# Plain block products for the first five feed-forward chunks, with the operand sums beside them

## The chip, the cores and the metric

One core of a Trainium2 chip runs the whole program in one launch. A time is the device time of that core in microseconds; the kernel before was timed three times, and once more under the profiler. Of the engines, TensorE (PE) multiplies matrices into PSUM, VectorE (DVE) and ScalarE (ACT) do the elementwise work, GpSimd (POOL) helps them, and SyncE (SP) issues nearly all transfers.

## What is computed

A two-layer encoder over two token streams (1024 and 256 tokens, each with 16 meta tokens ahead): layer 0 mixes tokens with a long convolution, layer 1 with attention. After each mixer comes a layer norm of the residual sum, and then the part that this change touches, a convolutional gated feed-forward block:

```python
def conv_ffn(x, w_in, conv_w, conv_b, w_out):
    h = x @ w_in                                  # 1024 -> 2 x 2816
    g, a = jnp.split(h, 2, axis=-1)
    g = dwconv3(g, conv_w, conv_b)                # width 3 over positions
    return (jax.nn.gelu(g, approximate=False) * a) @ w_out

def run_trunk(...):
    ...
        h = layer_norm(DEEPNORM_ALPHA * h + m, ln1_g[i], ln1_b[i])
        f = conv_ffn(h, ffn_w_in[i], ffn_conv_w[i], ffn_conv_b[i], ffn_w_out[i])
        h = layer_norm(DEEPNORM_ALPHA * h + f, ln2_g[i], ln2_b[i])
```

All is float32. The kernel keeps that accuracy by splitting each operand into a high and a low part (`split`: ScalarE rounds a copy, VectorE subtracts it) and adding three matmuls, high times high, high times low and low times high (`mm3`).

## The kernel before

Activations lie transposed, channels on partitions in 8 blocks of 128 (`KC`), tokens along the free axis. The tokens of both streams together are cut into four windows, which form two **pairs**: pair 0 has two windows of 384 tokens, pair 1 two of 272 (layer 0) or 258 (layer 1). A window carries one neighbour at each side for the convolution, so its matmuls have 386, 274 or 260 columns (`n2`). Within a pair the windows are c = 0 and c = 1.

**`out_proj`** is the mixer's output projection with the residual. For pair 0 and then pair 1 it takes 8 chunks `m` of 128 output channels, with 48 matmuls each, and adds the residual on VectorE. When a pair is through, its **`window_norms`** is put on a list of background generators. `tick(us)` runs a background generator on by one step whenever the foreground has emitted about that much matmul time; `need(key)` runs a generator to its end. So the list decides in which order work is *written*; each engine then executes its own queue in order. In the written order a recording layer makes small moves; where the result matters it is shown below.

`window_norms` normalises both windows of a pair (VectorE subtracts the mean and scales, ScalarE squares and adds the bias, GpSimd sums the squares, TensorE sums over partitions), stores them to `xd`, and makes the **operands** of the feed-forward product.

**`ffn_in`** computes `h` in 22 chunks of 128 hidden channels (`MF`); chunk m needs 128 columns of the gate half and 128 of the value half of `w_in`. For one pair that is a two by two block product: left the weight quarters a11, a12 (gate, input channels 0 to 511 and 512 to 1023) and a21, a22 (value), right the blocks B11, B21 (window 0, lower and upper channels) and B12, B22 (window 1). It is done with seven products in place of eight (`PRODUCTS`). The right operands are B11, B21, B22 and the sums T2, T1, T3, T4; the left ones are the quarters and sums of them, which `left_operands` forms on VectorE (four additions of 128x512 per chunk, L935 to L940) and splits (seven per chunk). A product has 4 blocks x 3 = 12 matmuls, so a chunk has 84 matmuls per pair. The products are added up partly in PSUM, partly by VectorE (L997, L1002, L1004) after a ScalarE copy (L995); then come the convolution (`conv3`, L315 to L317), Gelu, the multiplication by the value half and the store to `hd` (L989, L991).

The **order of chunks** is the list `jobs`. Chunks 0 to 3 (`FIRST = 4`) are done for pair 0 alone, then for pair 1 alone, and each of the two rounds loads and splits its weights for itself; chunks 4 to 21 are done for both pairs with one set of weights. While the first four run for pair 0, the ticks drive the norms and operands of pair 1.

Buffers that matter: weight quarters land in four tiles `raw`, their split parts take eight tiles `w`, so four split left operands exist at a time; `tp` has nine tiles, PSUM six banks for products. The stores, the loads of weights and the stores of normalised activations are all issued from SP's one queue. `ffn_out` follows and reads `hd` back.

## Time and profile before

| what | us |
|---|---|
| median of three runs (lowest to highest) | 3580.74 (3579.64 to 3582.94) |
| the profiled execution: its own time | 3577.93 |
| the profiled execution: span of the trace | 3575.6 |
| feed-forward input phase of layer 0, first to last matmul | 989.3 to 1584.8 |
| feed-forward input phase of layer 1, first to last matmul | 2631.1 to 3212.7 |

The page of the profile gives busy time by engine, then the span in 40 slices, then the transfer queues, the chain of work that ended last, and the costliest groups of instructions. A group's row has the source line, the engine, the operation, output and inputs by the program's names, shape and count, and then busy time and the mean of one in ns. In a timeline row the first two numbers are start and duration in us, and a bracket at the end gives how long the engine had been idle and what released it. A row of the stage view gives the stretch, its length, busy time of each engine with the number of instructions, the clock granted to TensorE (1.00 is full), and the transfer engines' share and rate. Matmuls overlap in the records: their cost in a row of them is the distance from start to start.

### The profile page before, as it was taken

What the parts mean: (1) busy time and instruction counts of PE and PEld (TensorE: products, weight loads), DVE (VectorE), ACT (ScalarE), POOL (GpSimd) and SP (SyncE); (2) the same over time, 40 slices, a digit from 0 to 9 for tenths busy, and PEclk for the clock granted to TensorE, in tenths of its full rate; (3) what the DMA queues carried; (4) which work ended last, traced back from release to release, by engine and by line L of the source; (5) the groups of instructions that cost most, each with busy time, mean ns of one, the idle gap of its engine ahead of it and who ended that gap; (6) DMA issues with size and microseconds to landing.
All of it is one profiled execution on the core that took longest, in us unless ns stands there. A gap on an engine that the chain in (4) does not pass through costs nothing.

```text
span 3575.6 us, 61608 instructions
## 1 busy us (share of the span) xinstructions
PE 3415.6 (96%) x23000; PEld 3307.6 (93%) x23000; DVE 2296.8 (64%) x4631; ACT 1708.4 (48%) x3614; POOL 523.8 (15%) x651
## 2 busy tenths in 40 slices
PE   8999999998989999999999999999988999999996
PEld 7999999998979999999999988888978999999996
DVE  6555554665797666654677557776499666664566
ACT  4333333663465444433455447777275444443454
POOL 2434341111110000000102341110110000000110
PEclk8999999999999999999999999999999999999998
DMA  5222223544223221236565440000233222227585
GB/s 167 94 94 95 91 83 120 145 134 149 93 85 99 63 75 62 75 125 212 169 212 166 140 141 16 14 14 25 92 114 100 67 74 64 75 82 227 165 224 141
DMA packets 236927, 391.72 MB, mean 110 GB/s; under 512 B 30580, under 2 KB 130139, under 8 KB 236243
## 3 DMA queue, kind: packets, MB, share of 16 engines
q1 hardware_dynamic: 228051, 359.38, 32.6%
q0 software_dynamic: 8576, 28.39, 2.2%
q8 instruction: 181, 2.97, 0.3%
q14 instruction: 119, 0.97, 0.1%
HBM read 302.22 MB, written 78.84 MB: 107 GB/s over the span
## 4 chain that ended last, share of the span: by engine, by line
PE 63%; DVE 6%; ACT 3%; DMA 3%; issue 1%; POOL 0%; SPq 0%; POOLq 0%; ACTq 0%; DVEq 0%
PE mm L288 17%; PE mm L290 17%; PE mm L289 17%; PE pt L1270 2%; DMA hraw<-hd 1%; PE sc L288 1%; DVE w L260 1%; PE pv L1286 1%; PE pv L1287 1%; PE pv L1288 1%; PE sc L289 1%; PE sc L290 1%; DVE T L260 1%; PE rs L1277 1%; DMA raw<-in_w_fin 1%
## 5 line engine op out<-in xcount | busy, mean ns | idle before, releaser
L288 PE MATMUL mm<-T,w 128*128 128x386 f32 (+2 forms) x2464 | 778.1, 316 | 34.0 <-ACT w L259 26.6
L290 PE MATMUL mm<-T,w 128*128 128x386 f32 (+2 forms) x2464 | 775.1, 315 | 3.9 <-DVE w L260 3.6
L260 DVE TENSOR_TENSOR w<-raw,w 128x512 fp32r<-128x512 f32 (+2 forms) x744 | 514.6, 694 | 410.7 <-ACT w L259 397.8
L289 PE MATMUL mm<-T,w 128*128 128x386 f32 (+2 forms) x2464 | 774.5, 314 | 0.0
L259 ACT CAST w<-raw 128x512 fp32r<-128x512 f32 (+2 forms) x744 | 438.9, 593 | 693.4 <-PE mm L289 531.8
L288 PE MATMUL mm<-y,w 128*128 128x386 f32 (+6 forms) x1664 | 545.4, 328 | 13.4 <-ACT y L259 9.4
L290 PE MATMUL mm<-y,w 128*128 128x386 f32 (+6 forms) x1664 | 532.0, 320 | 12.9 <-DVE w L260 12.8
L289 PE MATMUL mm<-y,w 128*128 128x386 f32 (+6 forms) x1664 | 533.4, 321 | 1.8 <-POOL y L260 1.1
L288 PEld LDWEIGHTS mm<-T,w 128*128 128x128 f32 x2464 | 468.3, 190 | 41.6 <-ACT w L259 31.1
L290 PEld LDWEIGHTS mm<-T,w 128*128 128x128 f32 x2464 | 468.0, 190 | 7.9 <-DVE w L260 7.7
L289 PEld LDWEIGHTS mm<-T,w 128*128 128x128 f32 x2464 | 468.9, 190 | 0.3
L288 PE MATMUL mm<-hq,w 128*128 128x328 f32 (+2 forms) x1408 | 441.2, 315 | 9.7 <-ACT hq L259 9.7
L289 PE MATMUL mm<-hq,w 128*128 128x328 f32 (+2 forms) x1408 | 441.3, 313 | 0.2
L290 PE MATMUL mm<-hq,w 128*128 128x328 f32 (+2 forms) x1408 | 441.0, 313 | 0.0
L790 POOL TENSOR_TENSOR tp<-tp,tp 128x384 f32<-128x384 f32 (+4 forms) x105 | 115.3, 1110 | 1753.7 <-ACT tp L788 1749.2
L288 PEld LDWEIGHTS mm<-y,w 128*128 128x128 f32 x1664 | 322.3, 194 | 18.4 <-ACT y L259 12.2
L290 PEld LDWEIGHTS mm<-y,w 128*128 128x128 f32 x1664 | 322.4, 194 | 14.5 <-DVE w L260 14.1
L289 PEld LDWEIGHTS mm<-y,w 128*128 128x128 f32 x1664 | 322.2, 194 | 7.9 <-DVE y L260 3.5
L288 PEld LDWEIGHTS mm<-hq,w 128*128 128x128 f32 x1408 | 266.7, 190 | 10.9 <-ACT hq L259 10.9
L289 PEld LDWEIGHTS mm<-hq,w 128*128 128x128 f32 x1408 | 267.9, 190 | 1.6 <-DVE hq L260 1.3
L290 PEld LDWEIGHTS mm<-hq,w 128*128 128x128 f32 x1408 | 267.5, 190 | 0.0
L260 DVE TENSOR_TENSOR hq<-hraw,hq 128x656 fp32r<-128x656 f32 (+1 forms) x220 | 188.8, 858 | 53.3 <-ACT hq L259 50.5
(213 smaller groups left out, 5770.8 us busy)
## 6 DMA issues: line engine op xcount, KB each, us to landing
raw<-in_w_fin SPq DMA_DIRECT2D x208, 256.0 KB
hraw<-hd SPq DMA_DIRECT2D x110, 328.0 KB
hraw<-hd SPq DMA_DIRECT2D x110, 321.0 KB
raw<-in_w_fout SPq DMA_DIRECT2D x88, 256.0 KB
hd<-g SPq DMA_DIRECT2D x88, 192.0 KB
raw<-in_w_fout SPq DMA_DIRECT2D x88, 192.0 KB
raw<-in_w_hin SPq DMA_DIRECT2D x48, 256.0 KB
kk<-kd SPq DMA_DIRECT2D x64, 192.0 KB
```

Source lines behind the costliest of these rows:

```text
L259: self.nc.scalar.copy(out=h, in_=src)
L260: (self.nc.gpsimd if pool else self.nc.vector).tensor_tensor(out=l, in0=src, in1=h, op=ALU.subtract)
L288: mm(out=ps, lhsT=wh, rhs=xh, start=start and i == 0, stop=False, **skip)
L289: mm(out=ps, lhsT=wh, rhs=xl, start=False, stop=False, **skip)
L290: mm(out=ps, lhsT=wl, rhs=xh, start=False, stop=stop and i == last, **skip)
L790: (adder or nc.gpsimd).tensor_tensor(out=sm, in0=sm, in1=sq, op=ALU.add)
L1270: nc.tensor.transpose(pt[:kn, q0:q0 + m], pr[:m, 128 * j:128 * j + kn], self.ident[:m, :m])
L1277: nc.tensor.matmul(out=rs[:, q0:q0 + m], lhsT=sm[:m, 3:4].to_broadcast([m, 128]), rhs=self.ident[:m, :m], start=True, stop=True)
L1286: mm(out=pv, lhsT=vh, rhs=ph[:kn, :nn], start=(jj == 0), stop=False)
L1287: mm(out=pv, lhsT=vh, rhs=pl[:kn, :nn], start=False, stop=False)
L1288: mm(out=pv, lhsT=vl, rhs=ph[:kn, :nn], start=False, stop=last)
```

## The change

Pair 0's first chunks are now five (`FIRST = 5`), and they are computed with **plain products**: gate and value rows, each for both windows, eight blocks of three matmuls into one bank, thus 4 x 24 = 96 matmuls per chunk. They need only B11, B21, B12 and B22 and no sums, on either side. Weight quarters are split as they come (`parts(quarter_of(...))`, four splits a chunk); the convolution reads PSUM directly, and nothing is added up outside PSUM.

`window_norms` of pair 0 therefore ends with 16 plain splits. The sums and splits for T2, T1 and T3 become a background generator of their own, `rest`, which runs by ticks during the five plain chunks; T4, which lies in the buffers of the activations (tag `y0`, where B12 was), is written after the fifth chunk (`end0`). Pair 1's norms and operands run in the background as before, with the same operations in another order.

Pair 1's chunks 0 to 4 no longer come in one row after pair 0's. `AFTER` puts each of them, alone, behind one of the chunks that are done for both pairs: chunk 0 behind 7, 1 behind 10, 2 behind 13, 3 behind 16, 4 behind 19. Chunks 5 to 21 are done for both pairs.

```diff
-FIRST = 4
+FIRST = 5
+AFTER = {FIRST + 2 + 3 * i: i for i in range(FIRST)}
...
+        if p == 0:
+            for x, src in (("B11", A[0][:4]), ("B21", A[0][4:]), ("B12", A[1][:4]), ("B22", A[1][4:])):
+                for k in range(4):
+                    if k % 2 == 0:
+                        operand(x, k // 2)
+                    put(x, k, src[k])
+                    yield 1
+
+            def rest():
+                for k in range(4):
+                    if k % 2 == 0:
+                        for x in ("T2", "T1", "T3"):
+                            operand(x, k // 2)
+                    sums(k)
+                    yield 3
+
+            def end():
+                for k in range(4):
+                    if k % 2 == 0:
+                        operand("T4", k // 2)
+                    put("T4", k, A[0][k + 4])
+                    yield 1
+
+            self.later("rest", rest())
+            self.end0 = end()
...
-        jobs = [(m, (p,)) for p in range(2) for m in range(FIRST)] + [(m, (0, 1)) for m in range(FIRST, MF)]
+        jobs = []
+        for m in range(FIRST, MF):
+            jobs.append((m, (0, 1)))
+            if m in AFTER:
+                jobs.append((AFTER[m], (1,)))

         def operands():
+            for m in range(FIRST):
+                for x in (w[m], w[MF + m]):
+                    yield 2, self.parts(self.quarter_of(x[:, 0:4])) + self.parts(self.quarter_of(x[:, 4:8]))
             for m, _ in jobs:
-                yield from self.left_operands(...)
+                for x in self.left_operands(...):
+                    yield 1, x
...
+        self.need(0)
+        for m in range(FIRST):
+            g = [self.tp(n) for _ in range(2)]
+            for row in range(2):
+                wt = weights()
+                for c, (x, y) in enumerate((("B11", "B21"), ("B12", "B22"))):
+                    ps = bank()[:, :n2]
+                    self.mm3(ps, [(*wt[k], *(z[:, k % 2] for z in T[x if k < 4 else y][k % 4 // 2])) for k in range(KC)])
+                    if row == 0:
+                        self.conv3(g[c], ps, n, self.cwf[:, l, m])
+                        nc.scalar.activation(out=g[c], in_=g[c], func=AF.Gelu)
+                    else:
+                        store(0, c, m, g[c], ps[:, 1:n + 1])
+                    self.tick(0.011 * n2)
+        self.need("rest")
+        for _ in self.end0:
+            pass
```

The order on the engines shows the move. **VectorE, layer 0, the last two chunks of pair 1's output projection.** T are right operands (T1905 and T1906 are high and low part of B11), A the normalised activations, tp sums, w the low parts of split weights (w1924 and w1927 before, w1910 and w1913 now, belong to output chunk 6), mm the product banks. Before:

```order
L260 TENSOR_TENSOR T1908_9580<-A1744_8477,T1907_9579 128x386
L906 TENSOR_TENSOR tp1920_9594<-A1752_8485,tp1919_9593 128x386
L260 TENSOR_TENSOR T1910_9582<-tp1919_9593,T1909_9581 128x386
L769 TENSOR_TENSOR tp1831_9042<-tp1831_9042,A1827_9038 128x274
L260 TENSOR_TENSOR T1912_9584<-tp1920_9594,T1911_9583 128x386
L911 TENSOR_TENSOR tp1919_9593<-A1744_8477,tp1919_9593 128x386
L260 TENSOR_TENSOR T1914_9586<-A1748_8481,T1913_9585 128x386
L260 TENSOR_TENSOR w1924_9642<-raw1922_9639,w1923_9641 128x512
L260 TENSOR_TENSOR T1916_9588<-A1752_8485,T1915_9587 128x386
L260 TENSOR_TENSOR w1927_9648<-raw1925_9645,w1926_9647 128x512
```

Now:

```order
L262 TENSOR_TENSOR T1906_9578<-A1740_8473,T1905_9577 128x386
L857 SCALAR_TENSOR_TENSOR A1827_9038<-A1827_9038,mm1907_9582 128x274
L262 TENSOR_TENSOR T1906_9578<-A1741_8474,T1905_9577 128x386
L771 TENSOR_TENSOR tp1831_9042<-tp1831_9042,A1827_9038 128x274
L262 TENSOR_TENSOR w1910_9614<-raw1908_9611,w1909_9613 128x512
L262 TENSOR_TENSOR T1916_9652<-A1742_8475,T1915_9651 128x386
L262 TENSOR_TENSOR w1913_9620<-raw1911_9617,w1912_9619 128x512
L262 TENSOR_TENSOR T1916_9652<-A1743_8476,T1915_9651 128x386
L262 TENSOR_TENSOR w1920_9688<-raw1918_9685,w1919_9687 128x512
```

Before, a whole block of sums and splits for the seven operands stood ahead of the two weight splits; now w1910 has two splits of B11 ahead of it, and w1913 one more.

**VectorE, layer 0, the first weights of the feed-forward block.** Before, with w1963 and w1965 for the first two products:

```order
L260 TENSOR_TENSOR T1944_9772<-tp1956_9831,T1943_9771 128x386
L260 TENSOR_TENSOR T1950_9778<-A1755_8488,T1949_9777 128x386
L260 TENSOR_TENSOR T1946_9774<-tp1957_9832,T1945_9773 128x386
L911 TENSOR_TENSOR tp1956_9831<-A1747_8480,tp1956_9831 128x386
L260 TENSOR_TENSOR w1963_9858<-raw1958_9849,w1962_9857 128x512
L935 TENSOR_TENSOR raw1960_9853<-raw1960_9853,raw1961_9855 128x512
L260 TENSOR_TENSOR T1952_9780<-tp1956_9831,T1951_9779 128x386
L260 TENSOR_TENSOR w1965_9862<-raw1959_9851,w1964_9861 128x512
```

Now, with w1942, w1945, w1948 and w1951 for the first chunk:

```order
L262 TENSOR_TENSOR T1937_9784<-A1754_8487,T1936_9783 128x386
L771 TENSOR_TENSOR tp1830_9041<-tp1830_9041,A1829_9040 128x274
L262 TENSOR_TENSOR T1937_9784<-A1755_8488,T1936_9783 128x386
L262 TENSOR_TENSOR w1942_9794<-raw1940_9791,w1941_9793 128x512
L904 TENSOR_TENSOR A1748_8481<-A1752_8485,A1748_8481 128x386
L262 TENSOR_TENSOR w1945_9800<-raw1943_9797,w1944_9799 128x512
L857 SCALAR_TENSOR_TENSOR A1829_9040<-A1829_9040,mm1927_9730 128x274
L262 TENSOR_TENSOR w1948_9806<-raw1946_9803,w1947_9805 128x512
L771 TENSOR_TENSOR tp1831_9042<-tp1831_9042,A1829_9040 128x274
L262 TENSOR_TENSOR w1951_9812<-raw1949_9809,w1950_9811 128x512
```

The first weight split was the 58th row from the first operand split (T1906) on and is now the 29th; the additions on `raw` are gone from this place.

**TensorE, layer 0, the start of the feed-forward block** (T1905, T1915 and T1925 are high parts of B11, B11 and B21). Before:

```order
L289 MATMUL mm1955_9795<-y993_5681,w1936_9735 128x274
L290 MATMUL mm1955_9795<-y985_5673,w1937_9736 128x274
L288 MATMUL mm1970_9875<-T1905_9577,w1962_9857 128x386
L289 MATMUL mm1970_9875<-T1906_9578,w1962_9857 128x386
L288 MATMUL mm1978_9912<-T1907_9579,w1964_9861 128x386
L290 MATMUL mm1970_9875<-T1905_9577,w1963_9858 128x386
L288 MATMUL mm1970_9875<-T1905_9577,w1962_9857 128x386
```

Now:

```order
L291 MATMUL mm1927_9730<-y993_5681,w1922_9693 128x274
L292 MATMUL mm1927_9730<-y985_5673,w1923_9694 128x274
L290 MATMUL mm1952_9815<-T1905_9577,w1941_9793 128x386
L291 MATMUL mm1952_9815<-T1906_9578,w1941_9793 128x386
L292 MATMUL mm1952_9815<-T1905_9577,w1942_9794 128x386
L290 MATMUL mm1952_9815<-T1905_9577,w1941_9793 128x386
L291 MATMUL mm1952_9815<-T1906_9578,w1941_9793 128x386
L292 MATMUL mm1952_9815<-T1905_9577,w1942_9794 128x386
L290 MATMUL mm1952_9815<-T1915_9651,w1941_9793 128x386
```

Before, the second product's first matmul was moved up between the first three; now one bank takes B11's and B21's 24 matmuls in a row.

More of the change, by code (lines that the diff above doesn't have):

```diff
@@ L882, in window_norms @@
                     yield x / 2
[L883 removed]
+        T = self.T[p] = {x: [None, None] for x in (*PRODUCTS, "B12")}
         left = 16
[L886 to L907 removed]
@@ new lines, in operand, with t, put @@
+        def operand(x, q):
+            def t():
+                nonlocal left
+                left -= 1
+                if left >= 0 or x == "T4" and p == 0:
+                    return self.act.tile([128, 2, n2], F32R, tag=f"y{p}", name=self.n("T"), bufs=16)
+                return self.tx.tile([128, 2, n2], F32R, tag=f"t{p}x", name=self.n("T"), bufs=(12, 16)[p])
+            T[x][q] = t(), t()
+        def put(x, k, src):
+            h, l = T[x][k // 2]
+            self.split(src, h[:, k % 2], l[:, k % 2])
@@ new lines, in window_norms @@
+        if p == 0:
[21 more added lines that the diff above has]
+        else:
+            for k in range(4):
+                if k % 2 == 0:
+                    for x in PRODUCTS:
+                        operand(x, k // 2)
+                put("B11", k, A[0][k])
+                put("B21", k, A[0][k + 4])
+                put("B22", k, A[1][k + 4])
@@ L908, in window_norms, with quarter_of, parts @@
                 yield 2
-                put("T3", b12)
-                put("B22", b22)
-                v.tensor_tensor(out=t2, in0=b21, in1=t2, op=ALU.subtract)
-                put("T4", t2)
+                sums(k)
+                put("T4", k, A[0][k + 4])
                 yield 2
+    def quarter_of(self, x):
+        r = self.quarter()
+        self.nc.sync.dma_start(out=r, in_=x)
+        return r
+    def parts(self, r):
+        h, l = self.part(), self.part()
+        self.split(r, h, l)
+        return [(h[:, k], l[:, k]) for k in range(4)]
@@ L920, in left_operands @@
         v = nc.vector
-        def load(x):
-            r = self.quarter()
-            nc.sync.dma_start(out=r, in_=x)
-            return r
-        def parts(r):
-            h, l = self.part(), self.part()
-            self.split(r, h, l)
-            return [(h[:, k], l[:, k]) for k in range(4)]
+        load, parts = self.quarter_of, self.parts
         r11, r12, r21, r22 = load(a11), load(a12), load(a21), load(a22)
@@ L970, in ffn_in @@
             for x in PRODUCTS:
-                while len(ready) < 4:
-                    r = next(ops, None)
-                    if r is None:
-                        break
-                    ready.append(r)
-                wt = ready.pop(0)
+                wt = weights()
                 for p in pairs:
```

55 lines of the change are left out of this document (26 added, 29 removed).

## The prediction

> **What bounds the kernel now.** I read the page's busy shares first, then the stages around the two feed-forward input phases, then the waits of TensorE and the rows around its idle times.
>
> ```profile
> span 3575.6 us, 61608 instructions
> PE 3415.6 (96%) x23000; PEld 3307.6 (93%) x23000; DVE 2296.8 (64%) x4631; ACT 1708.4 (48%) x3614; POOL 523.8 (15%) x651
> ```
>
> TensorE is busy 96% of the span, so on average nothing but fewer matmuls would help, and this change adds matmuls. But the share is an average. The stages of the input phase of layer 0, and two of layer 1 (columns: stretch, length, PE, PEld, DVE, ACT, POOL, granted clock, DMA share, GB/s), show where TensorE is not the bound:
>
> ```profile
> 940.00:980.00 40.00, 33.81 (x254) 33.58 (x253) 36.17 (x72) 24.92 (x51) 10.47 (x16) 0.88 0.41 145
> 980.00:1000.00 20.00, 13.18 (x83) 12.45 (x82) 19.27 (x41) 6.85 (x15) 0.00 (x0) 0.84 0.08 27
> 1020.00:1060.00 40.00, 30.77 (x151) 28.10 (x151) 39.60 (x96) 31.95 (x74) 1.86 (x24) 0.91 0.40 129
> 1400.00:1500.00 100.00, 100.00 (x661) 100.00 (x660) 61.61 (x115) 43.29 (x83) 0.00 (x0) 1.00 0.20 70
> 2620.00:2640.00 20.00, 12.97 (x89) 12.24 (x88) 19.61 (x44) 8.42 (x17) 0.00 (x0) 0.84 0.13 39
> 2660.00:2700.00 40.00, 31.43 (x160) 29.00 (x159) 39.55 (x97) 32.43 (x76) 1.85 (x24) 0.91 0.38 120
> ```
>
> From 980 to 1060 VectorE is full (19.27 of 20, 39.60 of 40) and TensorE has holes; from 1400 on it is the other way round. The clock is below 1 only where the holes are. Layer 1 repeats it. The timeline names the holes:
>
> ```profile
> 974.86 0.60 PE L290 MATMUL mm<-y,w 128*128 128x274 f32 x1 [6.19 <-DVE w L260]
> 996.00 0.69 PE L288 MATMUL mm<-T,w 128*128 128x386 f32 x1 [6.09 <-ACT w L259]
> 1031.20 0.45 PE L288 MATMUL mm<-T,w 128*128 128x386 f32 x1 [1.88 <-ACT tp L995]
> 1045.36 0.45 PE L288 MATMUL mm<-T,w 128*128 128x386 f32 x1 [3.78 <-ACT w L259]
> 2617.76 0.59 PE L290 MATMUL mm<-y,w 128*128 128x260 f32 x1 [6.41 <-DVE w L260]
> 2637.93 0.69 PE L288 MATMUL mm<-T,w 128*128 128x386 f32 x1 [6.30 <-ACT w L259]
> ```
>
> The first hole is in the output projection (its chunk 6 waits for its split weights), the second at the first feed-forward product, the rest in pair 0's four chunks. All wait for work that stands in VectorE's queue behind norms, sums and splits. What each part of the phase costs, by the matmuls of one line (PE, PEld, clock, DMA):
>
> ```profile
> 989.30:1079.00 89.70, 42.40 (x113) 23.22 (x113) 0.90 0.26 86
> 1079.00:1125.60 46.60, 32.89 (x113) 21.18 (x112) 1.00 0.36 118
> 1125.60:1584.80 459.20, 316.46 (x1008) 189.92 (x1007) 1.00 0.21 69
> 2630.60:2718.50 87.90, 41.89 (x115) 23.16 (x115) 0.92 0.27 86
> 2718.50:2765.00 46.50, 32.89 (x114) 21.25 (x113) 1.00 0.36 117
> 2765.00:3212.70 447.70, 311.96 (x1007) 189.74 (x1006) 1.00 0.22 70
> ```
>
> The rows of a layer are pair 0's four chunks, pair 1's four, and the 18 joint ones: 459.20 / 18 = 25.51 and 447.70 / 18 = 24.87 us per joint chunk. The steady price of a matmul is its distance to the next:
>
> ```profile
> 1580.94 0.34 PE L288 MATMUL mm<-T,w 128*128 128x386 f32 x1
> 1583.06 0.29 PE L288 MATMUL mm<-T,w 128*128 128x274 f32 x1
> 1584.48 0.28 PE L290 MATMUL mm<-T,w 128*128 128x274 f32 x1
> 2628.63 0.28 PE L288 MATMUL mm<-y,w 128*128 128x260 f32 x1
> 2631.00 0.28 PE L290 MATMUL mm<-y,w 128*128 128x260 f32 x1
> ```
>
> Twelve of 386 columns take 1583.06 - 1580.94 = 2.12, so 0.177 us each; 11 steps of 274 take 1.42 (0.129), 20 of 260 take 2.37 (0.119). Pair 0's four chunks are 336 matmuls, 59.4 us. They took 89.7, so 30.3 us were holes, half clock and norm matmuls.
>
> **The change part by part**, per layer.
>
> *Plain products.* Five chunks x 96 = 480 matmuls x 0.177 = 84.8 us; the seven-product way would be 420, so 60 more matmuls, 10.6 us, all on TensorE's path. VectorE gets lighter in return. Its prices:
>
> ```profile
> L260 DVE TENSOR_TENSOR w<-raw,w 128x512 fp32r<-128x512 f32 x55 | 40.7, 748 | 1.7 <-ACT w L259 1.4
> L935 DVE TENSOR_TENSOR raw<-raw,raw 128x512 f32<-128x512 f32 x7 | 5.4, 768 | 2.1 <-DMA raw<-in_w_fin 2.1
> L260 DVE TENSOR_TENSOR T<-A,T 128x386 fp32r<-128x386 f32 x16 | 8.9, 557 | 0.1
> L260 DVE TENSOR_TENSOR T<-A,T 128x274 fp32r<-128x274 f32 x16 | 6.7, 434 | 0.1
> L811 DVE SCALAR_TENSOR_TENSOR A<-A,lng,ln 128x274 f32<-128x274 f32 x16 | 6.9, 494 | 0.0
> L316 DVE SCALAR_TENSOR_TENSOR g<-tp,cwf,g 128x384 f32<-128x384 f32 x8 | 5.5, 684 | 0.8 <-ACT g L315 0.7
> ```
>
> A seven-product chunk costs VectorE seven splits and four additions (11 x 0.75 = 8.3) and nine operations of 386 columns (four of 0.68, five of 0.55: 5.5), 13.8 us beside 14.9 of TensorE. A plain one costs four splits (3.0), four convolution steps (2.7) and two multiplications (1.1), 6.8 beside 17.0. Five of them leave 5 x 10.2 = 51 us. What must fit in are pair 1's norms (16 x 0.43 + 16 x 0.49 = 14.7), its 28 splits and 16 sums (44 x 0.43 = 18.9), and pair 0's 16 sums and 16 splits put off (32 x 0.56 = 17.9): together 51.5 by the recorded durations. Those overlap: from start to start a 386 operation takes 0.47 in place of 0.55:
>
> ```profile
> 969.01 0.55 DVE L260 TENSOR_TENSOR T<-A,T 128x386 fp32r<-128x386 f32 x1
> 969.48 0.55 DVE L902 TENSOR_TENSOR A<-A,A 128x386 f32<-128x386 f32 x1
> 974.12 0.69 DVE L260 TENSOR_TENSOR w<-raw,w 128x512 fp32r<-128x512 f32 x1
> 974.72 0.56 DVE L260 TENSOR_TENSOR T<-A,T 128x386 fp32r<-128x386 f32 x1
> ```
>
> By these paces (0.47, 0.60 for 512, about a sixth less all through) it is 43 us in 57. So it fits, with a thin margin at first, since the order puts most of it beside the first two chunks. ScalarE has the same relief (four weight casts a chunk for seven).
>
> *Output projection.* The late split at 974.12 has moved up: from the first operand split at 969.0 (five rows: two of 386 columns at 0.47, two of 274 at 0.36, itself 0.60) it would be done at about 971.3, 3.5 us sooner. Before it ended at 974.8. I take 3.0 per layer, bounds 0 (the stores or the cast ahead hold it) and 6.2 (no hole).
>
> A hole of 2.6 us stays, and holes cost clock:
>
> ```profile
> 975.00:981.00 6.00, 6.00 (x27) 6.00 (x28) 5.35 (x12) 3.10 (x7) 0.00 (x0) 0.50 0.26 87
> 1031.00:1037.00 6.00, 5.80 (x24) 5.49 (x25) 5.60 (x13) 6.00 (x16) 0.93 (x12) 0.72 0.87 282
> ```
>
> After 6.19 us of idle the clock is 0.50 for six us; after the hole of 1.88 it is 0.72 over six. So I leave the half clock after 2.6 us as it was after 6.19. The Trainium skill ("TensorE: Matmul & The Clock Gate", section "What's actually happening") says that the clock halves after at least one idle window of about 3.4 us and comes back after as long a busy one. By that a hole of 2.6 us would be free, and each layer 3 us (half of six) better than my sum; the row of 1031 differs with the first half of it, and agrees with the second.
>
> *First feed-forward weights.* They were the 58th VectorE row from the first operand split on and are the 29th: about 13 us of queue in place of 27, done near 983, before the output projection ends near 986. The hole of 6.09 goes. What is late next are the splits of chunk 1. Eight `w` tiles now hold exactly one chunk, so chunk 1's first split must wait for the end of chunk 0's gate half, in the queues of ScalarE and VectorE, with norms behind it; its last split comes about when TensorE wants it. I take 2 us of holes, bounds 0 and 12 (the holes of before within these chunks, with their clock).
>
> *Norm matmuls* of pair 1 stay in this stage:
>
> ```profile
> L798 PE MATMUL ln<-squares,tp x12: 164/220/220, 1016.1 to 1019.1; 128*92 128x1 f32 x12
> L806 PE MATMUL ln<-squares,rs x12: 243/275/301, 1022.5 to 1026.9; 92*128 92x92 f32 x12
> ```
>
> At most 2.6 + 3.3 + 4 x 0.45 = 7.7, at least 0; matmuls advance by about half their recorded duration (0.177 for 0.34), so 3.
>
> *Stage sum.* 84.8 + 3 + 2 = 89.8 us for five chunks, where four took 89.7 (layer 0) and 87.1 (layer 1, 2631.1 to 2718.24).
>
> *One joint chunk fewer*: -25.5 and -24.9. *Five single chunks of pair 1 for four.* Steady they are 84 x 0.129 = 10.8 and 84 x 0.119 = 10.0; the four in a row took 46.60 / 4 = 11.65 and 11.62, since VectorE and the next weights barely keep pace. Between joint chunks (VectorE 62 of 100) they have more cover, but only four products can be split ahead. I take 11.2 and 10.8, so 56.0 - 46.6 = +9.4 and 54.0 - 46.5 = +7.5. The eight more weight transfers in all (a fifth single chunk's quarters, 256 KB each) hide where the DMA share is 0.21; SP's queue has stores among them, which wait for results that are ready. Uncovered they would be one landing each, some 3 us.
>
> *Sum.* Layer 0: -3.0 + 0.1 - 25.5 + 9.4 = -19.0. Layer 1: -3.0 + 2.7 - 24.9 + 7.5 = -17.7. Together -36.7, on the profiled execution's own 3577.93: 3541.2. That execution was 2.8 below the median, so in terms of the median 3580.7 - 36.7 = **3544 us**. Outside these phases the program is the same.
>
> **The rivals.**
>
> *The backlog stays.* The work taken off VectorE in pair 0's operands comes back beside chunks 0 and 1, with pair 1's norms. For it: the margin above is thin, and the order puts about 60 VectorE rows between the first weights and the last split of chunk 1. Against it: 60 rows at about 0.47 are 28 us, and from its start TensorE has 27.6 (17.0 + 8.5 + 2.1) until it wants that split, and VectorE starts on them some 3 us sooner. If each of four half chunks waits 3 us and pays 1.7 for the clock, it is 19 a layer in place of 2: -36.7 + 34 = -3, so 3578; half of that is 3561.
>
> *Everything fits.* No hole within the chunks, single chunks at the steady price, the first hole gone with its clock: -36.7 - 4 (holes) - 6 (singles) - 11 (2 x (2.6 + 3)) = -57.7, so 3523. For it: VectorE's total fits. Against: the queue's order.
>
> *The weight ring takes over, and it becomes slower.* One mechanism: with eight `w` tiles for two halves of a chunk, each half's splits can start only when the half before the last is through TensorE, and each must go through ScalarE's and VectorE's queues within one half, 48 x 0.177 = 8.5 us. From a queue delay of 8.5 on every half waits, ten a layer. It decides the sign when a half waits 1.8 us (36.7 / 20); at 3 us it is +60, so 3604. For it: before, VectorE's queue held a weight back by more than 20 us (996). Against: that was behind 57 rows; in the change two weight splits have at most 17 rows between them, some 8 us.
>
> *It does nothing*, because the holes are only moved: 3581. The 30 us of chunk 0 to 3 would have to come back whole; for that VectorE would have to be full for the whole 85 us. Its sum is 34 + 51.5 by the recorded durations, just that, but 71 by the paces at which it ran when it was full.
>
> **How the numbers follow.** The forecast (-20 to -50) 0.70, the backlog (-7 to -20) 0.13, everything fits 0.08, nothing 0.04, the ring 0.05. A difference under 0.2% (7 us) can't be told from none in this kernel. So faster 0.91, same 0.04, slower 0.05. The range runs from 3524 (where everything fits) to 3567 (two thirds of the backlog).
>
> **What would show it.** TensorE's first feed-forward matmul near 986 and 2628 with no hole of 6 us behind it; pair 0's five chunks done after about 90 us; the clock at 1.00 from then on; VectorE not full in the last two plain chunks; a single chunk at 10.0 to 11.6. Right for the wrong reason would be a gain with holes left in the plain chunks. Wrong it is if chunk 1 or 2 shows waits of several us for `w`, or if joint chunks next to single ones exceed 25.5.

## The result and the profile after

| | before | after |
|---|---|---|
| median, us (lowest to highest of four runs) | 3581.84 (3579.64 to 3583.41) | 3539.32 (3539.02 to 3543.38) |
| the profiled execution: its own time, us | 3577.93 | 3539.2 |
| the profiled execution: span, us | 3575.6 | 3537.2 |

The ratio of the times is 0.9884, with a 95% interval of 0.9871 to 0.9896: faster, as forecast. The medians differ by 42.5 us and the profiled executions by 38.7, where the sum was 36.7. The total agrees better than its terms do, so most of what follows is about the terms. The page's first lines of the kernel after:

```profile
span 3537.2 us, 61677 instructions
PE 3413.7 (97%) x23120; PEld 3317.4 (94%) x23120; DVE 2258.7 (64%) x4561; ACT 1687.8 (48%) x3572; POOL 531.3 (15%) x651
```

There are 120 more matmuls, 60 a layer, and TensorE's busy time is still 2 us less; VectorE has 38 us less to do. Neither number shows the 38.7 us; the holes do. The holes of TensorE between the last output projection and the output block, from the timeline (two of layer 0, the entry of layer 0's output block, and two of layer 1):

```profile
973.82 0.58 PE L292 MATMUL mm<-y,w 128*128 128x274 f32 x1 [2.73 <-DVE w L262]
1012.54 1.08 PE L800 MATMUL ln<-squares,tp 128*92 128x1 f32 x6 [3.12 <-POOL tp L792]
...
1574.17 0.84 PE L290 MATMUL mm<-hq,w 128*128 128x328 f32 x3 [4.57 <-ACT hq L261]
...
2597.22 0.38 PE L292 MATMUL mm<-y,w 128*128 128x260 f32 x1 [2.92 <-DVE w L262]
2634.87 0.63 PE L800 MATMUL ln<-squares,tp 128*88 128x1 f32 x6 [2.75 <-POOL tp L792]
```

The wait at the first feed-forward product (6.09 before) is gone, and so are the waits for `w` in the chunks behind it. The output projection keeps a shorter hole, 2.73 for 6.19. The wait on the output block was there before. What is new is the wait in the second row. It isn't a product that waits but a **norm matmul** of pair 1, the one that sums the squares over partitions, and it waits for **GpSimd**. The waits of TensorE, layer 0 from 940 to 1570 us (in total, times, longest):

```profile
PE ln L800 <- POOL tp L792: 3.1, 1, 3.1
PE mm L292 <- DVE w L262: 2.7, 1, 2.7
```

The same view of before has other names in it:

```profile
PE mm L288 <- ACT w L259: 13.1, 5, 6.1
PE mm L290 <- DVE w L260: 8.4, 7, 6.2
PE mm L288 <- ACT tp L995: 3.3, 3, 1.9
```

The stages after (stretch, length, PE, PEld, DVE, ACT, POOL, granted clock, DMA share, GB/s):

```profile
973.80:977.40 3.60, 3.58 (x16) 3.58 (x17) 3.18 (x6) 2.38 (x6) 0.00 (x0) 0.53 0.62 172
987.20:1020.00 32.80, 29.68 (x157) 29.17 (x156) 29.80 (x57) 19.97 (x42) 16.23 (x14) 0.90 0.22 69
1012.50:1018.50 6.00, 5.96 (x22) 5.96 (x23) 6.00 (x10) 3.65 (x10) 4.24 (x4) 0.52 0.12 46
1020.00:1060.00 40.00, 40.00 (x235) 40.00 (x234) 35.90 (x86) 28.28 (x64) 1.86 (x24) 1.00 0.47 149
1060.00:1081.30 21.30, 21.30 (x122) 21.30 (x121) 14.06 (x28) 8.53 (x18) 0.00 (x0) 1.00 0.16 53
1081.30:1500.00 418.70, 418.70 (x2807) 418.70 (x2807) 270.85 (x503) 189.98 (x365) 0.00 (x0) 1.00 0.23 74
2609.80:2702.50 92.70, 89.95 (x510) 89.48 (x509) 77.28 (x168) 56.31 (x123) 17.66 (x38) 0.98 0.31 96
```

Between 1020 and 1060, where before TensorE was busy 30.77 of 40 and VectorE 39.60, TensorE now is busy 40.00 at full clock. From 1081 on it has no hole either, single chunks included. The places that the terms are read from are the first feed-forward product of each layer, the first joint chunk, and a single chunk (its 84 matmuls of 274 columns and the 12 of the joint chunk ahead of it stand between the last two rows):

```profile
987.17 0.34 PE L290 MATMUL mm<-T,w 128*128 128x386 f32 x1
1081.32 0.34 PE L290 MATMUL mm<-T,w 128*128 128x386 f32 x1
...
2609.82 0.34 PE L290 MATMUL mm<-T,w 128*128 128x386 f32 x1
...
1156.50 0.29 PE L290 MATMUL mm<-T,w 128*128 128x274 f32 x1
1168.71 0.34 PE L290 MATMUL mm<-T,w 128*128 128x386 f32 x1
```

To compare runs I use one stretch, called the stage: from the first matmul of pair 1's output projection to the first matmul of the output block, in each layer. Before it is 662.39 and 646.18 us, after 644.99 and 627.21, thus 36.4 us less. The rest of the program took 2267.0 and 2265.0. The edits below leave it alone but for e11 and e12, and over their profiled executions it varies from 2265.0 to 2277.6 (span less stage). So a difference of a few us between two kernels is read from the stage; the whole time can't tell it. One thing stays open there: the rest was longest in e5, e8 and e6, which have fewer plain chunks (2271.9, 2274.6 and 2277.6, for 2265.0 to 2269.4 in after and in e1 to e4 and e10), and one profiled execution of each can't tell whether that belongs to these kernels.

The stage has a noise of its own. The output projection's hole, 2.73 and 2.92 us in after, is as long in e1 to e6, e8 and e10, but the clock behind it isn't (the last section has the rows). So the way from the stage's start to the first feed-forward product took 56.5 to 59.2 us in layer 0 and 54.0 to 56.8 in layer 1, even where the edit is far from it. The column "from the first product on" leaves this way out.

### The profile page after: what moved, and what is told of

Same layout as the page of the kernel before. It is cut to its first block, busy times and chain, and to the rows that moved or that the text cites. A ratio compares the mean times of both kernels' runs of the same rounds, so it can differ in the third digit from the quotient of the medians.

```text
span 3537.2 us, 61677 instructions
## 1 busy us (share of the span) xinstructions
PE 3413.7 (97%) x23120; PEld 3317.4 (94%) x23120; DVE 2258.7 (64%) x4561; ACT 1687.8 (48%) x3572; POOL 531.3 (15%) x651
## 4 chain that ended last, share of the span: by engine, by line
PE 69%; DVE 2%; ACT 2%; DMA 1%; issue 1%; POOL 1%; SPq 0%; POOLq 0%; ACTq 0%; DVEq 0%
PE mm L290 19%; PE mm L292 19%; PE mm L291 19%; PE pt L1335 2%; PE sc L290 1%; PE pv L1351 1%; PE pv L1352 1%; PE pv L1353 1%; PE sc L292 1%; PE sc L291 1%; DMA hraw<-hd 1%; PE rs L1342 1%; DMA qx<-qx 0%; DVE w L262 0%; PE ln L1171 0%
## 5 line engine op out<-in xcount | busy, mean ns | idle before, releaser
L290 PE MATMUL mm<-T,w 128*128 128x386 f32 (+2 forms) x2504 | 787.1, 314 | 0.0
L291 PE MATMUL mm<-T,w 128*128 128x386 f32 (+2 forms) x2504 | 785.1, 314 | 0.0
L292 PE MATMUL mm<-T,w 128*128 128x386 f32 (+2 forms) x2504 | 784.8, 313 | 0.0
L262 DVE TENSOR_TENSOR w<-raw,w 128x512 fp32r<-128x512 f32 (+2 forms) x728 | 501.2, 689 | 405.8 <-ACT w L261 391.8
L261 ACT CAST w<-raw 128x512 fp32r<-128x512 f32 (+2 forms) x728 | 429.3, 593 | 681.9 <-PE mm L291 538.0
L291 PEld LDWEIGHTS mm<-T,w 128*128 128x128 f32 x2504 | 474.3, 189 | 0.1
L290 PEld LDWEIGHTS mm<-T,w 128*128 128x128 f32 x2504 | 473.4, 189 | 0.1
L292 PEld LDWEIGHTS mm<-T,w 128*128 128x128 f32 x2504 | 473.5, 189 | 0.0
L290 PEld LDWEIGHTS mm<-y,w 128*128 128x128 f32 x1664 | 321.3, 193 | 20.2 <-ACT y L261 13.5
L290 PEld LDWEIGHTS mm<-hq,w 128*128 128x128 f32 x1408 | 266.4, 190 | 11.6 <-ACT hq L261 11.3
```

The source lines that it names most:

```text
L261: self.nc.scalar.copy(out=h, in_=src)
L262: (self.nc.gpsimd if pool else self.nc.vector).tensor_tensor(out=l, in0=src, in1=h, op=ALU.subtract)
L290: mm(out=ps, lhsT=wh, rhs=xh, start=start and i == 0, stop=False, **skip)
L291: mm(out=ps, lhsT=wh, rhs=xl, start=False, stop=False, **skip)
L292: mm(out=ps, lhsT=wl, rhs=xh, start=False, stop=stop and i == last, **skip)
```

## The experiments

All runs, sorted by what they are built on. "Stage" is the sum of both layers in the profiled execution, the ratio is the whole time against the kernel before on the same chip.

| run | stage, us | against its base | the same from the first product on | ratio (95%) |
|---|---|---|---|---|
| before | 1308.6 | | | 1 |
| e7, before, without pair 0's sums of weights | 1302.1 | -6.5 | -5.0 | 0.9988 (0.9979 to 0.9998) |
| e9, before, pair 1's operands at half pace | 1308.6 | 0.0 | +0.2 | 0.9995 (0.9986 to 1.0005) |
| after | 1272.2 | -36.4 against before | -27.5 | 0.9884 (0.9871 to 0.9896) |
| e1, after, variance matmuls later | 1264.5 | -7.7 | -6.0 | 0.9858 (0.9842 to 0.9874) |
| e2, after, sums of squares on VectorE | 1276.9 | +4.7 | +2.3 | 0.9883 (0.9867 to 0.9900) |
| e3, after, operand sums ahead of the chunks | 1286.6 | +14.4 | +13.4 | 0.9918 (0.9903 to 0.9933) |
| e4, after, single chunks in a row | 1282.1 | +9.9 | +13.0 | 0.9906 (0.9891 to 0.9921) |
| e5, after, four plain chunks | 1268.0 | -4.2 | -3.8 | 0.9878 (0.9860 to 0.9895) |
| e6, after, three plain chunks | 1278.7 | +6.5 | +8.1 | 0.9915 (0.9897 to 0.9933) |
| e8, after, e5 and e1 | 1258.7 | -13.5 | -10.5 | 0.9868 (0.9849 to 0.9887) |
| e10, after, 40 more VectorE operations a layer | 1294.7 | +22.5 | +21.4 | 0.9952 (0.9936 to 0.9969) |
| e11, e1 with the projection's weights a chunk earlier | 1266.1 | +1.6 against e1 | the edit is in the projection | 0.9879 (0.9864 to 0.9893) |
| e12, e8 with the same | 1262.1 | +3.4 against e8 | the edit is in the projection | 0.9878 (0.9863 to 0.9893) |

### The new wait: GpSimd's sums of squares (e1, e2)

In the norm ScalarE squares each of the 8 blocks into a `tp` tile, GpSimd adds them up one by one, and TensorE's variance matmul takes the result. GpSimd's additions, from 1000 to 1020 us of before and 990 to 1020 us of after (count, busy time, mean ns, idle time):

```profile
L790 POOL TENSOR_TENSOR tp<-tp,tp 128x274 f32<-128x274 f32 x14 | 13.6, 977 | 36.6 <-ACT tp L788 35.9
```

```profile
L792 POOL TENSOR_TENSOR tp<-tp,tp 128x274 f32<-128x274 f32 x14 | 16.2, 1165 | 31.9 <-ACT tp L790 31.3
```

One addition takes about 1 us, over twice what VectorE needs for one (0.45 in e2), and fourteen are 13.6 to 16.2 us. Before, this was hidden: TensorE stood 6.09 us at its first product meanwhile and reached its variance matmuls at 1016. Now it reaches them at 1009.4 (1012.54 - 3.12) and the sums aren't there. e1 leaves the sums alone and moves the matmuls 48 places later in TensorE's order; e2 leaves the order alone and takes GpSimd out.

```diff
 # e1
-        yield 8 + 2 * pace
+        yield gap + 2 * pace          # layer_norm(..., gap=8)
...
-        gens = [self.layer_norm(A[c], sms[c], idx, done(c)) for c in range(2)]
+        gens = [self.layer_norm(A[c], sms[c], idx, done(c), gap=16 if p else 8) for c in range(2)]
 # e2
+        gens = [self.layer_norm(A[c], sms[c], idx, done(c), adder=v if p else None) for c in range(2)]
```

> The changed kernel, with the variance matmuls of pair 1's layer norm written 48 matmuls (8.5 us) later in TensorE's queue, nothing else. Theory: the one hole left inside the five plain chunks (3.1 us in layer 0, 2.8 in layer 1, before those variance matmuls, released by GpSimd's sum of squares) is a matter of place in TensorE's queue; with 8.5 us more it is gone, and with it the half clock behind it (about 2 us): 4 to 5 us a layer, 3530 to 3532 us against 3539 for the change. Rival: what stands later in the queues (pair 1's scaling and operands, 8.5 us later) comes back as a wait of the first joint chunk: then no gain, 3539 or more, and a hole near 1080.

> The changed kernel, with the 14 additions of squares of pair 1's norm on VectorE in place of GpSimd (28 in both layers). Theory: GpSimd's pace of 1.17 us per addition makes the hole before the variance matmuls; on VectorE an addition takes 0.36 to 0.43, so the hole goes, at 5 to 6 us more of VectorE beside chunks 0 and 1: 3530 to 3535 us. Rival: VectorE is so full there that its weight splits come late in place of it: holes released by w, 3539 to 3545.

The holes that e1 has in the place of the wait on GpSimd (layer 0 and 1), and those of e2 (layer 0):

```profile
1016.54 0.45 PE L292 MATMUL mm<-T,w 128*128 128x386 f32 x1 [1.65 <-DVE w L262]
...
2633.63 0.44 PE L292 MATMUL mm<-T,w 128*128 128x386 f32 x1 [1.48 <-DVE w L262]
```

```profile
1015.82 0.65 PE L800 MATMUL ln<-squares,tp 128*92 128x1 f32 x6 [1.86 <-DVE tp L792]
1018.30 0.44 PE L292 MATMUL mm<-T,w 128*128 128x386 f32 x1 [1.83 <-DVE w L262]
```

In e1 the wait on GpSimd is gone, the stage is 7.7 us shorter, and half of the old wait stays as one on a split weight. The five plain chunks took 90.1 and 90.0 us, for 94.15 and 92.7 in after. So that wait, with its clock, had a net cost of 4.0 and 2.7 us, and another place of the matmuls in TensorE's queue is enough to take it away. In e2 the sums stand in VectorE's queue, which is full there, and two waits of 1.86 and 1.83 take the place of one. The stage is 4.7 us longer, but half of that lies ahead of the first product, where the clock behind the projection's hole was lower; from there on it is 2.3 us. The rival was right that nothing is gained (0.9883 for 0.9884) and that holes at `w` come. GpSimd is slow, but VectorE has no room for this work there.

### What removed the wait at the first product (e3)

The prediction gave the loss of the 6 us hole to the order of VectorE's queue: the operand sums moved from ahead of the first weights to behind them. e3 keeps the plain products and writes the sums ahead again.

```diff
-            self.later("rest", rest())
+            yield from rest()
```

> The changed kernel, with pair 0's sums and their splits (28 VectorE rows) written ahead of the first plain chunk again and not beside the chunks; the plain products and all else stay. Theory: the gain at the start of the phase comes from what stands ahead of the first feed-forward weights in VectorE's queue: these weights move back by 19 to 31 rows, 9 to 14 us, so a hole of 7 to 11 us opens at the first feed-forward matmul, with 2 to 3 us of half clock, while the hole at the variance matmuls (5 us with its clock) may shrink: 3550 to 3562 us. Rival: the light plain weights alone make the gain and the place of the sums does not matter: within 4 us of 3539.

```profile
997.33 0.69 PE L292 MATMUL mm<-T,w 128*128 128x386 f32 x1 [7.37 <-DVE w L262]
...
2630.57 0.69 PE L292 MATMUL mm<-T,w 128*128 128x386 f32 x1 [11.44 <-DVE w L262]
```

The hole is back, 7.37 and 11.44 us, and the wait on GpSimd isn't there any more: TensorE comes later again, and GpSimd is faster too (its additions have a mean of 0.830 us). The stage is 14.4 us longer, about 40% of the gain (13.4 from the first product on). The theory held: with the plain products alone and the sums in their old place, the first weights stay behind them.

### Single chunks, in a row or spread (e4)

```diff
-        jobs = []
-        for m in range(FIRST, MF):
-            jobs.append((m, (0, 1)))
-            if m in AFTER:
-                jobs.append((AFTER[m], (1,)))
+        jobs = [(m, (1,)) for m in range(FIRST)] + [(m, (0, 1)) for m in range(FIRST, MF)]
```

> The changed kernel, with pair 1's five single chunks in a row right behind the plain chunks and not among the joint ones. Theory: a single chunk costs 11.65 us in a row, as before the change, and its steady 10.7 and 10.0 among joint chunks: +4.9 us in layer 0 and +7.9 in layer 1, so 3550 to 3553 us. Rival: before the change the four in a row were slow because of what the norms had left over on VectorE, which is done sooner now: then no difference, 3539 to 3542.

The five in a row took 57.19 and 58.92 us, thus 11.44 and 11.78 each, close to the 11.65 and 11.49 of before. Spread they take 12.21 us for 96 matmuls (1156.50 to 1168.71), so 10.68 for 84; in layer 1 11.48 for 96, so 10.05. That is 0.127 and 0.120 us a matmul, the steady price. In a row they wait in small pieces such as

```profile
1102.42 0.39 PE L290 MATMUL mm<-T,w 128*128 128x274 f32 x1 [0.84 <-ACT tp L1056]
...
2751.75 0.47 PE L290 MATMUL mm<-T,w 128*128 128x260 f32 x1 [1.85 <-ACT w L261]
```

By these prices spreading is worth 3.8 us in layer 0 ((11.44 - 10.68) x 5) and 8.7 in layer 1 ((11.78 - 10.05) x 5); by the stage it is 1.3 and 8.7. What is missing in layer 0 lies ahead of the single chunks: up to the first product e4 took 56.49 us, for 57.99 in after, and in the plain chunks 93.10 for 94.15, with the same holes and a higher clock behind them (1.00 and 0.72 over six us, for 0.72 and 0.52). Behind the plain chunks e4 loses 3.8 and 8.6 us, which are the prices.

### How many plain chunks (e5, e6, e8)

```diff
 # e5                # e6
-FIRST = 5          -FIRST = 5
+FIRST = 4          +FIRST = 3
```

> The changed kernel with four plain chunks and not five (and four single chunks of pair 1). Theory: a plain chunk costs 12 matmuls of 386 columns more than seven products, 2.1 us; VectorE had its operands done some 18 us ahead of the first joint chunk, one plain chunk is 17, so four suffice nearly: 2.1 us a layer less, 3535 us. Rival: VectorE doesn't get through in four, and the first joint chunk waits for pair 1's operands or its weights: 3540 to 3550, with a hole near 1067.

> The changed kernel with three plain chunks. Theory: 4.2 us of matmuls a layer are saved, but VectorE's operands end some 16 us after the third chunk, so the first joint chunk waits about that long, less what it does meanwhile: 3539 - 8 + 2 x (10 to 17 with the clock) = 3551 to 3565 us. Rival: the number of plain chunks pays only in matmuls: 3531.

With four chunks only the two known holes are left in layer 0's stage, and the stage is 4.2 us shorter. The price of the fifth chunk by steady paces is 96 x 0.177 + 10.7 - 25.5 = 2.2 us in layer 0, about that again in layer 1. With three, the first joint chunk comes too early for its operands and weights:

```profile
1056.14 0.40 PE L291 MATMUL mm<-T,w 128*128 128x274 f32 x1 [1.00 <-DVE T L262]
1061.54 0.69 PE L290 MATMUL mm<-T,w 128*128 128x386 f32 x1 [4.87 <-ACT w L261]
...
2689.32 0.69 PE L290 MATMUL mm<-T,w 128*128 128x386 f32 x1 [4.75 <-ACT w L261]
```

That costs more than the chunk saved: the stage is 6.5 us longer than with five, 3.6 and 2.9 us a layer where 6 to 13 were expected (the whole time, 3556 us, lies in the range expected). So four is the least number tried that covers pair 1's norms and operands. In the whole time e5 (0.9878) can't be told from five (0.9884). e8 puts e5 and e1 together:

> Four plain chunks and the variance matmuls of pair 1's norm 48 matmuls later, both. If the two are independent it is the sum of both: 3527 us with 2.1 and 4.5 us a layer. Rival: with the norm finished 8.5 us later and one chunk less of cover, the first joint chunk waits, and it is no better than the better one of the two alone.

The stage is 13.5 us shorter than that of the change, where the two alone give 4.2 + 7.7 = 11.9; from the first product on it is 10.5 for 3.8 + 6.0 = 9.8. So they add up. It has the shortest stage of all runs. The whole time, 3536 us, is not the 3527 expected. Whole times don't separate it from e1: 0.9868 (0.9849 to 0.9887) and 0.9858 (0.9842 to 0.9874).

### How far VectorE was the limit (e7, e9, e10)

The prediction's main argument was a total: the plain chunks take 51 us from VectorE, and about that much has to fit in. Three runs test it. e7 is the kernel before, without the four additions on weights in pair 0's four chunks (the sums of left operands are left out, so the products use the quarters in their places); nothing else is moved. e9 is the kernel before with pair 1's operands at half the pace. e10 is the change with two maxima of each weight quarter with itself in the plain chunks, 40 operations or about 24 us a layer, so that a plain chunk costs VectorE some 11.6 us in place of 6.8 (the maxima give the quarter itself).

```diff
 # e7 (before): left_operands(..., add) with add = False in the first FIRST jobs
+        if add:
             v.tensor_tensor(out=r21, in0=r21, in1=r22, op=ALU.add)
...
 # e9 (before), twice in the operand loop
-                yield 2
+                yield 4 if p else 2
 # e10 (after), for each quarter z of the plain chunks
+                        for _ in range(2):
+                            v.tensor_tensor(out=z, in0=z, in1=z, op=ALU.max)
```

> The kernel before the change, without the four additions on the weight quarters in pair 0's first four chunks (left out: the left-hand sums there, 16 VectorE operations of 0.60 to 0.69 us a layer; the splits and matmuls stay, on wrong numbers). Theory: VectorE's queue sets the time from 969 to 1062, so 9.6 us of it taken away are worth about as much, 8 to 12 us a layer: 3558 to 3566 us against 3581. Rival: the holes come from the ring of weight tiles and from landing times; then it gives under 2 us a layer, 3577 or more.

> The kernel before the change, where only the pace changes at which pair 1's operands are written among pair 0's four chunks: a step every 4 us of matmul time and not every 2; VectorE has the same operations. Theory, formed after the run without left sums gave only some 1.5 us a layer: not the amount of VectorE work made the holes in these chunks, but that a block of norm and operand work stood ahead of weight splits that TensorE wanted sooner; spread out, the holes of 3.8 and 2.4 us and their half clock go, 3 to 8 us a layer: 0.9955 to 0.998 of the time before. Rival: the amount of VectorE work decides: no gain, or some us lost behind the fourth chunk, where pair 1's chunks need the rest of the operands.

> The changed kernel with eight more VectorE operations of 128x512 in each plain chunk (each weight quarter is replaced twice by its maximum with itself, which leaves it as it is): 4.8 us more a chunk, so that a plain chunk's weights load VectorE as much as those of seven products. Theory, that the place in the queue decides: VectorE has some 18 us to spare over the five chunks and 24 us are added, about half of it beside chunks 0 and 1, which are tight: 3 to 8 us a layer, 0.990 to 0.993 of the time before. Rival, that the plain weights' lightness makes the gain: most of it goes, 0.996 or more.

**e7** takes 16 x 0.60 = 9.6 us off VectorE in each layer and wins 2.9 and 3.6 us of the stage, 1.6 and 3.3 from the first product on. The theory fell; the rival, under 2 us, has the size of layer 0 alone. Two of its holes, and then three stages of e7 and the same three of before:

```profile
998.24 0.69 PE L288 MATMUL mm<-T,w 128*128 128x386 f32 x1 [6.11 <-ACT w L259]
...
1057.85 0.69 PE L288 MATMUL mm<-T,w 128*128 128x386 f32 x1 [3.56 <-ACT w L259]
```

```profile
1000.00:1020.00 20.00, 19.03 (x96) 18.38 (x96) 16.40 (x32) 14.86 (x33) 12.48 (x14) 0.87 0.18 53
1020.00:1040.00 20.00, 17.49 (x104) 16.52 (x103) 16.92 (x42) 19.30 (x41) 2.73 (x25) 1.00 0.58 174
1040.00:1060.00 20.00, 14.32 (x64) 12.84 (x62) 20.00 (x51) 14.56 (x36) 0.00 (x0) 0.82 0.28 82
```

```profile
1000.00:1020.00 20.00, 18.79 (x107) 18.07 (x106) 18.98 (x37) 16.76 (x35) 13.55 (x14) 0.96 0.16 53
1020.00:1040.00 20.00, 18.12 (x98) 17.38 (x98) 19.60 (x48) 19.94 (x47) 1.86 (x24) 0.91 0.57 185
1040.00:1060.00 20.00, 12.64 (x55) 10.72 (x55) 20.00 (x49) 12.00 (x28) 0.00 (x0) 0.90 0.22 72
```

The time won goes to idle time of VectorE between 1000 and 1040 (16.40 and 16.92 of 20, for 18.98 and 19.60), where GpSimd's sums and pair 1's norm are under way. After 1040, when the norm lets pair 1's operands follow, VectorE is full (20.00 of 20), and TensorE waits. The hole at the first product (6.11) is as it was. So VectorE isn't short of time as such; it is short of it in certain stretches.

**e9** moves the holes and changes nothing in the sum. One that it has in each layer:

```profile
1069.35 0.44 PE L288 MATMUL mm<-T,w 128*128 128x386 f32 x1 [3.85 <-ACT tp L995]
...
2710.37 0.69 PE L288 MATMUL mm<-T,w 128*128 128x386 f32 x1 [3.77 <-ACT tp L995]
```

The rival was right that nothing is gained. Spreading the same work within the same stretch is not enough; the stretch holds too much of it.

**e10** loses 22.5 us of the 36.4, 11.3 a layer for 24 us of operations: more than the 3 to 8 of the theory, less than the rival's (0.9952 lies between the two). Three of its holes, at the two halves of chunk 1 in layer 0 and at the second half of chunk 1 in layer 1, and two stages:

```profile
1006.44 0.45 PE L290 MATMUL mm<-T,w 128*128 128x386 f32 x1 [1.34 <-ACT w L261]
1024.95 0.69 PE L290 MATMUL mm<-T,w 128*128 128x386 f32 x1 [3.98 <-ACT w L261]
...
2662.02 0.69 PE L290 MATMUL mm<-T,w 128*128 128x386 f32 x1 [4.60 <-ACT w L261]
```

```profile
985.00:1028.00 43.00, 33.38 (x169) 31.25 (x170) 40.63 (x76) 22.39 (x45) 13.60 (x14) 0.88 0.16 52
1028.00:1060.00 32.00, 32.00 (x178) 32.00 (x178) 29.66 (x68) 22.68 (x51) 1.84 (x24) 0.95 0.47 154
```

Layer 0's holes are in the first 43 us, with VectorE at 40.63, but for one of 1.33 us in the fifth chunk (at 1081.85); in the 32 us behind the first 43 TensorE is busy throughout, although the plain chunks there carry the same additional work. So the light weights of the plain chunks are needed, and mostly beside the first two chunks.

### The hole in the output projection (e11, e12)

The 2.7 us hole before the last output chunks is the wait for a split weight. e11 (on e1) and e12 (on e8) write the load and splits of the next chunk's weights one window earlier.

```diff
-                wt = self.next if m == 0 and self.next else self.load_w(w[m])
+                wt = self.next or self.load_w(w[m])
...
+                    if c == 0 and m + 1 < KC:
+                        self.next = self.load_w(w[m + 1])
```

> The changed kernel with the variance matmuls later, as in the run of that alone (0.9858 of the time before), and the output projection's weights split one chunk ahead, so that the splits for its sixth chunk stand among the 16 scaling operations and not behind them. Theory: the hole of 2.7 us there is the place of those two splits in VectorE's queue; it goes, with 2 to 3 us of half clock behind it: about 4 to 5 us a layer less, 0.983 to 0.984. Rival: the hole moves to the first plain chunk, whose weights or operands come later by the same work: 0.9855.

> All three together: four plain chunks, the variance matmuls later, the projection's weights one chunk ahead. If each gives what its own run gave within the phase (3.9 us for four plain chunks over both layers), it is 4 us under the kernel with five: about 0.982. Rival: with four chunks there's no time left for pair 1's operands when TensorE is never held up before: no better than with five, and a wait at the first joint chunk.

```profile
987.91 0.62 PE L292 MATMUL mm<-T,w 128*128 128x386 f32 x1 [2.66 <-DVE w L262]
...
2609.38 0.69 PE L292 MATMUL mm<-T,w 128*128 128x386 f32 x1 [3.57 <-DVE w L262]
```

The hole in the projection is gone, and one of 2.66 and 3.57 us stands at the first feed-forward product (these rows are e11's; e12 has the same two waits). The rival was right: what VectorE does earlier for the projection delays the next weights. In e11 the way to the first product is 4.4 and 3.7 us shorter than in e1, and the plain chunks are 4.5 and 5.5 longer. The stage is 1.6 and 3.4 us longer than without.

## Why the prediction was right, and where its terms were off

Read from the stage, by layer (plain chunks from the first feed-forward product to the first joint or single chunk, each end at its first matmul; in before these are 89.39 and 87.12 us for pair 0's four chunks, 46.58 and 45.94 for pair 1's):

| term | forecast, layer 0 / 1 | measured, layer 0 / 1 |
|---|---|---|
| output projection | -3.0 / -3.0 | -4.6 / -4.2 |
| plain chunks | +0.1 / +2.7 | +4.8 / +5.6 |
| one joint chunk fewer | -25.5 / -24.9 | -24.4 / -24.7 |
| single chunks | +9.4 / +7.5 | +6.8 / +4.3 |
| sum | -19.0 / -17.7 | -17.4 / -19.0 |

**The output projection.** The mechanism was right: fewer rows ahead of the split, and a hole of 2.73 and 2.92 us left where 2.6 was worked out. No run moves these rows alone. The size was off at "So I leave the half clock after 2.6 us as it was after 6.19". It is half for 3.6 us (0.53 in the row of 973.80), not for six, which gives back 1.2 us; another 0.5 is what 3.0 was taken under the 3.5 worked out. This size is luck of the execution: in e2 the same hole has six us at 0.50 behind it, as the prediction had it, and in e4 none (rows in the last section). A hole of 2.73 us did cost the clock here. By the Trainium skill ("TensorE: Matmul & The Clock Gate", section "What's actually happening") the clock halves only after an idle window of about 3.4 us, which these rows differ with; that it comes back after as long a busy one agrees with the 3.6 us of this row; in e2 it took six.

**The first feed-forward weights.** Right in place and reason. The first product came at 987.17, where "near 986" stood, with no hole behind it, and e3 shows that the order of VectorE's queue is the cause.

**The plain chunks.** This is the step that failed: "What is late next are the splits of chunk 1." No product waited for a weight in chunk 1. The variance matmul of pair 1's norm waited 3.12 and 2.75 us for GpSimd, which the prediction had as 3 us of norm matmuls with no wait, and in none of its rivals. The 94.15 us are 84.8 of products, 3.1 of the hole, 2.9 of half clock behind it (the row of 1012.50, six us at 0.52), and 3.3 for the rest, norm matmuls among it, where 3 was forecast for these. The 2 us allowed for holes were meant for something else and were 4.0 us short with the clock (2.5 in layer 1). e1 shows the cause: with this wait out of the way the plain chunks take the 90 us that were forecast, and the weight waits that the prediction expected do come up, at 1.65 us. The prediction called a gain with holes left in the plain chunks right for the wrong reason; for this one term that is so.

**The single chunks.** The direction was right, the size was not: "11.2 and 10.8" was chosen between the steady price and that of four in a row, and the steady price was measured (10.68 and 10.05). In layer 1 the price in a row was also read too high: the four took 45.94 us from first matmul to first matmul, not 46.5. e4 shows that it is the spreading that does it. The doubt about "only four products can be split ahead" was unfounded beside joint chunks.

**The joint chunk** had its price; the 1.1 and 0.2 us that are missing are spread over the other 17, which also hold the output block's wait (4.57 for 4.39).

**VectorE's total.** The conclusion "it fits" was right: the last operand of pair 1 was ready about 17 us before the first joint chunk began, and e5 shows that one chunk fewer fits too. But the argument by totals isn't what decides. e7 gave VectorE 9.6 us and won 1.6 and 3.3 from the first product on, e9 changed the pace and won nothing, e10 took 24 us and lost 11.3, nearly all in the first chunks. What decided is what stands in the queue in the first 40 us of the block, and the change lightens just that: the sums of weights and of operands both go from there.

**The rivals.** Of "the ring" there is no sign: no wait on a half of a chunk in after. "Everything fits" had the singles right and missed the norm; e8, at 13.5 us less by the stage, is two thirds of the way to it (it stood 21 us under the forecast), in part by one plain chunk fewer, which that rival didn't have. That the sum came so near is partly luck: projection and single chunks gave 8.6 us more than forecast, plain and joint chunks 8.9 less. The clock behind the projection's hole alone could have made it 2.4 us less, as in e2, or 3.0 more, as in e4.

The better version is e1 or e8. Both are small edits to the change, and from the first product on they gain another 0.2 and 0.3% (6.0 and 10.5 of 3539 us). In whole times they are 0.9858 and 0.9868 for 0.9884, with intervals that overlap.

## What to carry to other kernels

When a stall is taken away, ask of every instruction on the freed engine's queue what it needs and how long the slowest helper takes for that; the next wait stood on GpSimd, in a chain that nobody had waited for before. Don't add up an engine's work over a stage: a queue in order makes late what stands behind it, so put light work where the queue is full, and test it by adding or removing work in that stretch alone. Where unchanged parts of a program vary by some 13 us between executions, measure a small change by its own stage, and look there too for holes that the change leaves alone but behind which the clock differs.

## What was unexpected in the hardware

VectorE and GpSimd slow each other. While GpSimd adds squares, six VectorE operations of 386 columns take twice their time. Others beside it keep theirs, as those from 1002.66 to 1005.70, and then it is GpSimd's addition that takes long. Two VectorE rows of the kernel after, one inside GpSimd's work and one behind it, and that addition, where the first of the 14 took 0.78:

```profile
1010.74 1.12 DVE L262 TENSOR_TENSOR T<-tp,T 128x386 fp32r<-128x386 f32 x1
...
1019.14 0.55 DVE L262 TENSOR_TENSOR T<-tp,T 128x386 fp32r<-128x386 f32 x1
```

```profile
1002.66 3.68 POOL L792 TENSOR_TENSOR tp<-tp,tp 128x274 f32<-128x274 f32 x1 [3.84 <-ACT tp L790]
```

In e2, with nothing on GpSimd, the same operations of VectorE take 0.56. GpSimd's own additions have a mean of 0.977 us in before, 1.165 in after, and 0.830 in e3 (layer 0), where pair 0's sums are done ahead of them. The Trainium skill ("SBUF — State Buffer", section "Who interferes with whom") says that a VectorE instruction with two inputs in SBUF contends with a GpSimd instruction that reads SBUF; these rows agree. So the 14 additions cost more than their own 16 us: six VectorE operations of 386 columns took 1.11 to 1.12 in place of 0.55, some 3.4 us of the fullest stretch of VectorE's queue. The other way, the 3.68 us stand in the chain of additions that TensorE's wait of 3.12 us ended on, so a part of that wait may be VectorE's doing. What either is worth wasn't tried; e2, which takes GpSimd out, puts the 14 additions into VectorE's queue.

The clock behind one and the same hole differs from run to run. Over the six us behind the projection's 2.73 us of layer 0 it was 0.50 in e2 and e5, 0.72 to 0.74 in after, e1, e3 and e6, and 1.00 in e4, e8 and e10. The rows of e2 and of e4:

```profile
971.70:977.70 6.00, 5.97 (x26) 5.97 (x27) 3.73 (x8) 2.40 (x6) 0.00 (x0) 0.50 0.63 186
```

```profile
971.90:977.90 6.00, 5.96 (x46) 5.96 (x47) 5.96 (x13) 4.10 (x10) 0.00 (x0) 1.00 0.61 187
```

Layer 1's 2.92 us cost as differently (0.72 in after, 0.50 in e2, e3 and e10, 1.00 in the others). Behind the 6.2 and 6.4 us of before, e7 and e9 it was 0.50 to 0.77 each time. So a hole of under 3 us costs its own length or up to 3 us more; no run here shows what decides.
